# Turning the last row block of the MLP's input by transposing DMAs, in two halves of its columns

## The chip, the core and the metric

The kernel runs on one core of a Trainium2 chip. The metric is the time of one execution on the device in microseconds (us); shorter is better. An engine does its instructions in a fixed order, which is set when the kernel is built. TensorE (PE in the profile) multiplies, with its weight loads shown apart as PEld; VectorE is DVE, ScalarE is ACT, GpSimd is POOL, and SyncE (SP) issues most of the DMAs. "SPq" and "POOLq" mark the issuing side of a DMA.

## The reference

One layer of an encoder on 512 tokens of 1024 channels in float32: two attention branches, a gated merge, an output projection and a layer norm, then a gated MLP with a causal convolution of width 3. The change lies at the border between the first norm and the MLP:

```python
x = layer_norm(DEEPNORM_ALPHA * x + merged @ w_out[layer], ln1_g[layer], ln1_b[layer])
u, g = jnp.split(x @ w_ffn_in[layer], 2, axis=-1)
h = jax.nn.gelu(causal_dwconv(u, conv_w[layer], conv_b[layer])) * g
x = layer_norm(DEEPNORM_ALPHA * x + h @ w_ffn_out[layer], ln2_g[layer], ln2_b[layer])
```

## The kernel before

**Split products.** Every float32 matrix that is multiplied is held as a high part rounded to TensorE's fast float32 form (names ending in `h` or `hi`) and a low part, the rest (`l`, `lo`). A product is three matmuls: high by high, high by low, low by high. The high part is a ScalarE copy, the low part a VectorE subtraction.

**The border.** The output projection `out_proj` (lines 862 to 872) and the norm `first_norm` (lines 874 to 884) go over four row blocks of 128 tokens, j = 0 to 3, with tokens on the partitions. The MLP wants channels on the partitions: `x1h` and `x1l` hold the turned input, 8 chunks of 128 channels by 512 tokens. So each block has to be transposed.

Blocks 0 to 2 are turned by DMAs. A transposing DMA here takes 2-byte elements, so `send` (lines 903 to 910) copies the upper and the lower 16 bits of each number apart into `own` (two ScalarE copies of 128 x 1024) and SyncE issues one transposing DMA for each into `got`. `join` (lines 912 to 919) puts the halves of the numbers together in `back` (two ScalarE copies), and splits it into `x1h` (ScalarE) and `x1l` (VectorE). Block j is joined while the next block is projected.

Block 3 has no next block. `turn(3)` (lines 886 to 896) transposes it by eight TensorE matmuls against the identity (line 892) into two PSUM tiles `xt_ps`, and `x1h` and `x1l` are split straight from there.

**The MLP.** Its input weights come in 44 pieces of 128 output channels: u0, g0, u1, g1, ... (`f` counts them, u and g of one `f` belong together). A piece is 8 chunks x 3 matmuls = 24 matmuls of 512 tokens (`ffn_in`, lines 936 to 942). A piece's weights are loaded by SyncE into one of three raw tiles, and split into one of three pairs `whi`, `wlo` by ScalarE (line 104) and VectorE (line 113); a pair comes free when the piece has been multiplied. `activate(f)` evacuates u (ScalarE), convolves it (VectorE, lines 985 to 987), applies the GELU (ScalarE) and multiplies by g (VectorE). After every second `f` `first_products` begins the second matrix product, in accumulators P, Q and R, with weight pieces dx and dy that VectorE first adds and subtracts (lines 963 to 966).

Since block 3 comes last, the MLP starts on tokens 0 to 255 (`t_lo`), which need blocks 0 and 1 only: u0 whole, then six chunks of g0, then the transposes of block 3, two chunks of g0, and then u0 and g0 on tokens 256 to 511 (`t_hi`). u1 and all later pieces take 512 tokens at once. A program that simulates the times orders the instructions of each engine within the dependencies; `issue_after` ties one instruction behind another.

After the norm of block 3 has read its scale and offset, GpSimd loads those of the second norm into the same two tiles (`ln2` and `ln3`, line 828, 512 KB each).

Of the kernel before, what the change touches and what calls it, by code (L numbers as in the profile page):

```python
# [48 lines left out]
def r32(ap):  # L49
    return ap.bitcast(F32)  # L50
# [77 lines left out]
def tile_block(ctx: ExitStack, tc: tile.TileContext, xT, xN, w_qi, w_ki, w_t, w_v, w_br, w_o, w_fi, w_fo,  # L128
               bg, cw, rel, onehot, lnp, out):
    nc = tc.nc  # L130

    def close(p):
        p.__exit__(None, None, None)
# [69 lines left out]
    st = Stream(tc, rawp, ring, order, 3, 3, place, POOL_LO, DMA_LO)  # L203
# [4 lines left out]
    ps = pb("idle_ps")  # L208
# [4 lines left out]
    ident = cst.tile([128, 128], F32, name="ident")  # L213
# [86 lines left out]
    for k in range(KC):  # L300
# [9 lines left out]
        for n in range(4):  # L310
            c = slice(n * 128, n * 128 + 128)
# [360 lines left out]
    for a, b in ((0, 512), (512, NREL)):  # L672
        ps = pa("line_ps")
# [136 lines left out]
    for p in range(4):  # L810
        wh_wl = st.get(f"ba{p}")
        for n in (2 * p, 2 * p + 1):
            if n not in early and n not in gps:
                gps[n] = whole(proj_t(f"ga{n}"))
            ps = pb("ba_ps")
            wh, wl = wh_wl
            for k in range(4):
                c = slice((n % 2) * 512 + k * 128, (n % 2) * 512 + k * 128 + 128)
# [21 lines left out]
    def norm_apply(dst, r, mv, rstd, g, b, c):  # L840
        nc.vector.scalar_tensor_tensor(dst[:, c], r[:, c], mv[:, 0:1], g[:, c], op0=ALU.subtract, op1=ALU.mult)
        return nc.vector.scalar_tensor_tensor(dst[:, c], dst[:, c], rstd, b[:, c], op0=ALU.mult, op1=ALU.add).ins


    g1, b1 = bcast(0, "lg"), bcast(1, "lb")
# [8 lines left out]
    x1 = [dp.tile([128, D], F32, tag="r", bufs=NB, name=f"r{j}") for j in range(NB)]  # L854
# [3 lines left out]
    x1h = qp.tile([128, KC, S], F32R, name="x1h")  # L858
    x1l = qp.tile([128, KC, S], F32R, name="x1l")
# [14 lines left out]
    def first_norm(j, pss):  # L874
        r = x1[j]
        parts = padded(dp, [128, 2, 6], tag="parts", bufs=2, name="parts")
        for nh in range(2):
            c = slice(nh * 512, nh * 512 + 512)
            nc.vector.scalar_tensor_tensor(r[:, c], r[:, c], ALPHA, pss[nh], op0=ALU.mult, op1=ALU.add)
            nc.vector.bn_stats(parts[:, nh], r[:, c])  # L880
        mv, rstd = norm_stats(r, parts)
        for nh in range(2):
            last = norm_apply(r, r, mv, rstd, g1, b1, slice(nh * 512, nh * 512 + 512))
        return last

    def turn(j):
        t0 = slice(j * 128, j * 128 + 128)
        for nh in range(2):
            ps = pb("xt_ps")
            for k in range(4):  # L890
                kk = nh * 4 + k
                turned_last = nc.tensor.transpose(ps[:, k * 128:k * 128 + 128], x1[j][:, kk * 128:kk * 128 + 128], ident)
            src = ps.rearrange("p (k t) -> p k t", k=4)
            nc.scalar.activation(x1h[:, nh * 4:nh * 4 + 4, t0], src, AF.Copy)
            nc.vector.tensor_sub(x1l[:, nh * 4:nh * 4 + 4, t0], src, r32(x1h[:, nh * 4:nh * 4 + 4, t0]))
        return turned_last.ins

    tpc, tp = open_pool("tp", reuse_waits="tile")

    def halves_of(t):  # L900
        return t.bitcast(U16).rearrange("p (c two) -> p two c", two=2)

    def send(j):
        own = tp.tile([128, 2, D], U16, tag="own", bufs=1, name=f"own{j}")
        got = tp.tile([128, 2, KC, 128], U16, tag="got", bufs=1, name=f"got{j}")
        src = halves_of(x1[j])
        for a in (1, 0):
            nc.scalar.activation(own[:, a], src[:, a], AF.Copy)
            nc.sync.dma_start_transpose(got[:, a], own[:, a])
        return got  # L910

    def join(j, got):
# [17 lines left out]
    ec, ep = open_pool("ep", reuse_waits="tile")  # L930
# [5 lines left out]
    def ffn_in(w, ps, c, chunks=range(KC), lows_last=0):  # L936
        wh, wl = w
        terms = [(k, a, b) for k in chunks for a, b in ((wh, x1h), (wh, x1l), (wl, x1h))]
        terms.sort(key=lambda t: (t[0] >= lows_last, t[2] is x1l and t[0] < lows_last))
        for n, (k, a, b) in enumerate(terms):  # L940
            nc.tensor.matmul(ps[:, c], a[:, k * 128:k * 128 + 128], b[:, k, c], start=(k == 0 and a is wh and b is x1h),  # L941
                             stop=(n == len(terms) - 1 and k == KC - 1))
# [37 lines left out]
    def activate(f, ups, gps_):  # L980
        u = padded(fp, [128, S + 2], tag="u", bufs=2, name="u")
        nc.gpsimd.memset(u[:, 0:2], 0.0)  # L982
        nc.scalar.activation(u[:, 2:S + 2], ups, AF.Copy)
        c = fp.tile([128, S], F32, tag="c", bufs=2, name="c")
        nc.vector.tensor_scalar(c, u[:, 0:S], cwt[:, f, 0:1], None, op0=ALU.mult)
        nc.vector.scalar_tensor_tensor(c, u[:, 1:S + 1], cwt[:, f, 1:2], c, op0=ALU.mult, op1=ALU.add)
        nc.vector.scalar_tensor_tensor(c, u[:, 2:S + 2], cwt[:, f, 2:3], c, op0=ALU.mult, op1=ALU.add)  # L987
        nc.scalar.activation(c, c, AF.Gelu_apprx_tanh, bias=cwt[:, f, 3:4])  # L988

        if f % 2 == 0:  # L990
            hidden["F"] = hp.tile([128, 7, 256], F32, tag="F", bufs=1, name="hF")
            hidden["a"] = (hp.tile([128, 3, 256], F32R, tag="ah", bufs=1, name="ah"),
                           hp.tile([128, 3, 256], F32R, tag="al", bufs=1, name="al"))
        F = hidden["F"]
        o = 2 + 2 * (f % 2)
        nc.vector.tensor_mul(F[:, o:o + 2].rearrange("p a b -> p (a b)"), gps_, c)  # L996
        ah, al = hidden["a"]
        if f % 2 == 0:
            nc.scalar.activation(ah[:, 2], F[:, 2], AF.Copy)
            nc.vector.tensor_sub(al[:, 2], F[:, 2], r32(ah[:, 2]))  # L1000
            return
        nc.vector.tensor_add(F[:, 0], F[:, 3], F[:, 5])
        nc.vector.tensor_sub(F[:, 1], F[:, 0], F[:, 2])
        nc.scalar.activation(ah[:, 0:2], F[:, 0:2], AF.Copy)
        nc.vector.tensor_sub(al[:, 0:2], F[:, 0:2], r32(ah[:, 0:2]))
        nc.vector.tensor_sub(F[:, 3], F[:, 2], F[:, 3])
        nc.vector.tensor_sub(F[:, 6], F[:, 4], F[:, 1])
        bh = ep.tile([128, 4, 256], F32R, tag="bh", bufs=NP, name=f"bh{f//2}")
        bl = ep.tile([128, 4, 256], F32R, tag="bl", bufs=NP, name=f"bl{f//2}")
        nc.scalar.activation(bh, F[:, 3:7], AF.Copy)  # L1010
        nc.vector.tensor_sub(bl, F[:, 3:7], r32(bh))
        if f < FC - 1:
            first_ops.append((ah, al))
        rest_ops.append((bh, bl))
# [19 lines left out]
    early_w = {}  # L1034

    full, t_lo, t_hi = slice(0, S), slice(0, 256), slice(256, 512)
    w0 = [st.get("u0"), st.get("g0")]
    ps0 = [pa("u_ps"), pa("g_ps")]
    ffn_in(w0[0], ps0[0], t_lo)
    ffn_in(w0[1], ps0[1], t_lo, range(6))  # L1040
    with tc.issue_after(turn(NB - 1)):
        ffn_in(w0[1], ps0[1], t_lo, range(6, KC))
    ffn_in(w0[0], ps0[0], t_hi, lows_last=4)
    ffn_in(w0[1], ps0[1], t_hi)
    u1_ps = pa("u_ps")
    ffn_in(st.get("u1"), u1_ps, full)
    activate(0, *ps0)
    g1_ps = pa("g_ps")
    ffn_in(st.get("g1"), g1_ps, full)
    activate(1, u1_ps, g1_ps)  # L1050
    close(ac)
    psc, psC = open_pool("psC", space=PSUM, reuse_waits="tile")
    psd, psD = open_pool("psD", space=PSUM, reuse_waits="tile")
# [8 lines left out]
    for f in range(2, FC):  # L1062
        ups = bank_c("u_ps")
        ffn_in(st.get(f"u{f}"), ups, full)
        if f % 2 == 0:
            i = f // 2 - 1
            early_w[i] = st.get(f"dx{i}"), st.get(f"dy{i}")
            if i == 0:
                Q += [pb(f"Q{a}") for a in range(2)]
                R += [pb(f"R{a}") for a in range(2)]  # L1070
            first_products(i, (P, Q, R))
            if i < NB:
                nc.scalar.activation(x1[i], x1[i], AF.Copy, scale=ALPHA)
# [81 lines left out]
    i = NP - 1  # L1155
# [148 lines left out]
```

## Time and profile before

| | |
|---|---|
| median of three runs | 744.62 us (744.21 to 745.03) |
| profiled execution | 744.63 us |
| its span, first to last instruction | 742.8 us |
| mean granted TensorE clock | 0.998 |
| TensorE busy | 734.1 us, 99% of the span |
| VectorE, ScalarE, GpSimd busy | 570.8, 407.4, 150.2 us |
| DMA traffic | 117.03 MB |

The rows of a timeline give start and duration of an instruction in us, the engine, the line of the kernel, the operation, what it writes and from what, the shape, and in brackets the idle time of its engine before it and what ended it. Matmuls overlap: the time that one costs is the distance from its start to the next one's. The rows by tile give least, median and greatest duration in ns. A row of windows gives for a stretch the busy time of each engine, the granted clock, the mean busy share of the 16 DMA engines and GB/s.

### The profile page before, as it was taken

The page shows a single profiled execution, that of the slowest core. Times are in us where ns is not written, and L with a number is a line of the kernel's source. Part 1 is how long each engine was busy: PE and PEld are TensorE (multiplying, and loading weights), DVE is VectorE, ACT ScalarE, POOL GpSimd, SP SyncE. Part 2 cuts the span into 40 slices and gives each one's busy share as a digit, 9 for nine tenths or more (in the row PEclk, how much of TensorE's full clock was granted, in tenths as well). Part 3 has the DMA queues.
Part 4 walks back from the last instruction along what each step waited for, and adds up shares of the span by engine and source line. Part 5 has one row for each costly group of instructions (what it writes and reads, how often), then busy time and mean ns, then how long its engine had stood idle before and what let it go on. Part 6 is the DMA issues. An engine that isn't in the chain of part 4 may idle for free.

```text
span 742.8 us, 9709 instructions
## 1 busy us (share of the span) xinstructions
PE 734.1 (99%) x3453; PEld 615.3 (83%) x3453; DVE 570.8 (77%) x907; ACT 407.4 (55%) x572; POOL 150.2 (20%) x161
## 2 busy tenths in 40 slices
PE   9999999999999999999999999999999999999995
PEld 7888888888888888888889888888888888888885
DVE  5569888999679898668856776686767677668985
ACT  6466867797685688755384443443344344345430
POOL 0001224365753341000101111011101101110011
PEclk9999999999999999999999999999999999999999
DMA  8445887797476454438633535344443444448532
GB/s 266 158 123 183 200 191 167 153 214 171 120 184 163 135 138 124 121 114 268 236 62 116 168 114 169 120 143 147 159 141 114 158 141 154 140 145 285 193 117 86
DMA packets 73631, 117.03 MB, mean 158 GB/s; under 512 B 42536, under 2 KB 42792, under 8 KB 73584
## 3 DMA queue, kind: packets, MB, share of 16 engines
q1 hardware_dynamic: 66304, 93.98, 42.0%
q0 software_dynamic: 5744, 18.38, 9.9%
q10 hardware_dynamic: 1536, 4.06, 2.1%
q8 instruction: 27, 0.44, 0.2%
q14 instruction: 20, 0.16, 0.1%
HBM read 95.93 MB, written 9.98 MB: 143 GB/s over the span
## 4 chain that ended last, share of the span: by engine, by line
PE 98%; DVE 1%; issue 0%; DVEq 0%
PE u_ps L941 16%; PE g_ps L941 16%; PE av_ps L512 3%; PE m L1021 2%; PE m L1022 2%; PE m L1020 2%; PE ga_ps L234 2%; PE ga_ps L235 2%; PE ga_ps L233 2%; PE gb_ps L235 2%; PE gb_ps L233 2%; PE gb_ps L234 2%; PE o_ps L870 2%; PE o_ps L869 2%; PE o_ps L868 2%; PE z_ps L540 1%
## 5 line engine op out<-in xcount | busy, mean ns | idle before, releaser
L104 ACT ACTIVATE whi<-raw 128x1024 fp32r<-128x1024 f32 (+1 forms) x124 | 123.6, 1000 | 141.5 <-PE g_ps L941 45.0
L113 DVE TENSOR_TENSOR wlo<-raw,whi 128x1024 fp32r<-128x1024 f32 (+1 forms) x105 | 123.3, 1177 | 39.2 <-ACT whi L104 38.5
L941 PE MATMUL g_ps<-x1h,whi 128*128 128x512 f32 (+1 forms) x184 | 70.0, 380 | 0.0
L941 PE MATMUL g_ps<-x1l,whi 128*128 128x512 f32 (+1 forms) x184 | 69.9, 380 | 0.0
L941 PE MATMUL g_ps<-x1h,wlo 128*128 128x512 f32 (+1 forms) x184 | 69.9, 380 | 0.0
L941 PE MATMUL u_ps<-x1h,wlo 128*128 128x512 f32 (+1 forms) x184 | 69.8, 380 | 0.0
L941 PE MATMUL u_ps<-x1h,whi 128*128 128x512 f32 (+1 forms) x184 | 69.7, 380 | 0.0
L941 PE MATMUL u_ps<-x1l,whi 128*128 128x512 f32 (+1 forms) x184 | 69.3, 380 | 0.0
L941 PEld LDWEIGHTS u_ps<-x1h,wlo 128*128 128x128 f32 x184 | 34.6, 188 | 6.6
L941 PEld LDWEIGHTS g_ps<-x1l,whi 128*128 128x128 f32 x184 | 34.6, 188 | 6.6
L941 PEld LDWEIGHTS g_ps<-x1h,wlo 128*128 128x128 f32 x184 | 34.6, 188 | 6.6
L941 PEld LDWEIGHTS g_ps<-x1h,whi 128*128 128x128 f32 x184 | 34.6, 188 | 6.5
L941 PEld LDWEIGHTS u_ps<-x1h,whi 128*128 128x128 f32 x184 | 34.6, 188 | 6.4
L941 PEld LDWEIGHTS u_ps<-x1l,whi 128*128 128x128 f32 x184 | 34.4, 188 | 6.7
L963 DVE TENSOR_TENSOR t<-raw 128x512 f32<-128x512 f32 x11 | 7.6, 692 | 37.0 <-DMA raw<-in_w_fo_dram 37.0
L569 POOL TENSOR_TENSOR bm<-win,score 128x256 f32<-128x256 f32 (+2 forms) x24 | 28.9, 1229 | 31.9 <-DMA pl<-bm 21.8
L996 DVE TENSOR_TENSOR hF<-g_ps,c 128x512 f32<-128x512 f32 x22 | 15.1, 688 | 21.9 <-PE g_ps L941 21.1
L988 ACT ACTIVATE c<-c,cwt 128x512 f32<-128x512 f32 x22 | 15.9, 724 | 29.0 <-DVE c L987 28.8
L982 POOL MEMSET u<- 128x2 f32 x22 | 2.1, 98 | 147.3 <-ACT whi L104 111.1
L837 POOL TENSOR_TENSOR rstd<-rstd,mhalf 128x1 f32<-128x1 f32 x8 | 7.7, 958 | 104.5 <-DVE rstd L836 104.5
L424 DVE MAX8 m<-score 128x8 f32<-128x256 f32 (+2 forms) x48 | 26.6, 556 | 1.0
L557 POOL TENSOR_TENSOR beta<-beta,keep 128x1280 f32<-128x1280 f32 x8 | 21.0, 2626 | 26.9 <-DVE keep L554 26.9
(576 smaller groups left out, 2086.6 us busy)
## 6 DMA issues: line engine op xcount, KB each, us to landing
raw<-in_w_fi_dram SPq DMA_DIRECT2D x44, 512.0 KB, 3.3
raw<-in_w_t_dram SPq DMA_DIRECT2D x32, 512.0 KB, 3.8
raw<-in_w_fo_dram SPq DMA_DIRECT2D x26, 512.0 KB, 3.8
wlo<-in_w_t_dram POOLq DMA_DIRECT2D x14, 512.0 KB, 5.9
raw<-in_w_br_dram SPq DMA_DIRECT2D x8, 512.0 KB, 3.7
raw<-in_w_o_dram SPq DMA_DIRECT2D x8, 512.0 KB, 3.6
raw<-in_w_v_dram SPq DMA_DIRECT2D x7, 512.0 KB, 4.4
raw_b<-in_w_fo_dram SPq DMA_DIRECT2D x6, 512.0 KB, 4.2
```

The source lines that it names most:

```text
L104: self.high = nc.scalar.activation(hi[:, :w], t[:, :w], AF.Copy).ins
L113: self.done[key] = eng.tensor_sub(lo[:, :w], t[:, :w], r32(hi[:, :w])).ins
L233: nc.tensor.matmul(ps[:M], wh[:, c], xh[k], start=(k == 0), stop=False)
L234: nc.tensor.matmul(ps[:M], wh[:, c], xl[k], start=False, stop=False)
L235: ups["proj"] = nc.tensor.matmul(ps[:M], wl[:, c], xh[k], start=False, stop=(k == KC - 1)).ins
L424: nc.vector.max(m8, sc)
L512: nc.tensor.matmul(dst, vt[i][:, h].rearrange("p a d -> p (a d)"), t, start=(n == 0), stop=(n == len(seq) - 1))
L557: nc.gpsimd.tensor_mul(beta, beta, keep[:, 1:ATT + 1])
L569: nc.gpsimd.tensor_add(bm[:, OFF[j]:OFF[j] + N], win[:, 512 - N:512], score[j])
L941: nc.tensor.matmul(ps[:, c], a[:, k * 128:k * 128 + 128], b[:, k, c], start=(k == 0 and a is wh and b is x1h), stop=(n == len(terms) - 1 a ...
L988: nc.scalar.activation(c, c, AF.Gelu_apprx_tanh, bias=cwt[:, f, 3:4])
L996: nc.vector.tensor_mul(F[:, o:o + 2].rearrange("p a b -> p (a b)"), gps_, c)
```

## The change

Block 3 is now turned by transposing DMAs as well, in two halves of 512 columns. `first_norm` finishes the first half of the columns and hands it to `send_half`, then the second. `send_half` copies the upper 16 bits by ScalarE and the lower ones by VectorE and issues two transposing DMAs of 128 x 512. `join_half` puts a half together (the upper bits by ScalarE, the lower by VectorE) and splits it into four chunks of `x1h` and `x1l`.

u0, g0 and u1 now all take tokens 0 to 255 first, and then tokens 256 to 511, chunks 0 to 3 of all three before chunks 4 to 7. So u1 is 48 matmuls of 256 tokens in place of 24 of 512.

```diff
         mv, rstd = norm_stats(r, parts)
-        for nh in range(2):
-            last = norm_apply(r, r, mv, rstd, g1, b1, slice(nh * 512, nh * 512 + 512))
+        cols = [slice(nh * 512, nh * 512 + 512) for nh in range(2)]
+        if j < NB - 1:
+            for c in cols:
+                last = norm_apply(r, r, mv, rstd, g1, b1, c)
+            return last
+        for c in cols:
+            nc.vector.scalar_tensor_tensor(r[:, c], r[:, c], mv[:, 0:1], g1[:, c], op0=ALU.subtract, op1=ALU.mult)
+        last = None
+        for nh, c in enumerate(cols):
+            with tc.issue_after(last) if last is not None else nullcontext():
+                nc.vector.scalar_tensor_tensor(r[:, c], r[:, c], rstd, b1[:, c], op0=ALU.mult, op1=ALU.add)
+            last = send_half(j, nh)
         return last
...
+    def send_half(j, nh):
...
+        nc.scalar.activation(own[:, 1, c], src[:, 1, c], AF.Copy)
+        low = nc.vector.tensor_copy(own[:, 0, c], src[:, 0, c]).ins
+        for a in (1, 0):
+            nc.sync.dma_start_transpose(got[:, a, 4 * nh:4 * nh + 4], own[:, a, c])
+        return low
+
+    def join_half(j, nh, got, back, after):
...
+            nc.scalar.activation(halves_of(raw)[:, 1], got[:, 1, k].rearrange("p b c -> p (b c)"), AF.Copy)
+            nc.vector.tensor_copy(halves_of(raw)[:, 0], got[:, 0, k].rearrange("p b c -> p (b c)"))
+        src = raw.rearrange("p (k t) -> p k t", k=4)
+        high = nc.scalar.activation(x1h[:, k, t0], src, AF.Copy).ins
+        low = nc.vector.tensor_sub(x1l[:, k, t0], src, r32(x1h[:, k, t0])).ins
+        return high, low
...
-    w0 = [st.get("u0"), st.get("g0")]
-    ps0 = [pa("u_ps"), pa("g_ps")]
-    ffn_in(w0[0], ps0[0], t_lo)
-    ffn_in(w0[1], ps0[1], t_lo, range(6))
-    with tc.issue_after(turn(NB - 1)):
-        ffn_in(w0[1], ps0[1], t_lo, range(6, KC))
-    ffn_in(w0[0], ps0[0], t_hi, lows_last=4)
-    ffn_in(w0[1], ps0[1], t_hi)
-    u1_ps = pa("u_ps")
-    ffn_in(st.get("u1"), u1_ps, full)
-    activate(0, *ps0)
+    w0 = [st.get(t) for t in ("u0", "g0", "u1")]
+    ps0 = [pa(f"{t}_ps") for t in ("u", "g", "u")]
+    for w, ps in zip(w0, ps0):
+        ffn_in(w, ps, t_lo)
+    for chunks in (range(4), range(4, KC)):
+        for n, (w, ps) in enumerate(zip(w0, ps0)):
+            ffn_in(w, ps, t_hi, chunks, lows_last=4 if n == 0 else 0)
+    activate(0, *ps0[:2])
```

**The order on TensorE, where the tokens 256 to 511 begin.** Before; whi_3460 and wlo_3461 are u0's weights, whi_3466 g0's, whi_3472 and wlo_3473 u1's:

```order
L941 MATMUL g_ps<-x1h,wlo_3467 128x256
L892 MATMUL xt_ps<-ident,r_3479 128x128 x8
L941 MATMUL g_ps<-x1h,whi_3466 128x256
L941 MATMUL g_ps<-x1l,whi_3466 128x256
L941 MATMUL g_ps<-x1h,wlo_3467 128x256
```

In the changed kernel, at the first matmul that reads block 3 (the second row) and a little behind it:

```order
L972 MATMUL u_ps<-x1h,wlo_3473 128x256
L972 MATMUL u_ps<-x1h,whi_3460 128x256
L972 MATMUL u_ps<-x1h,wlo_3461 128x256
L972 MATMUL u_ps<-x1h,whi_3460 128x256
L972 MATMUL u_ps<-x1h,wlo_3461 128x256
L972 MATMUL u_ps<-x1h,whi_3460 128x256
L972 MATMUL u_ps<-x1h,wlo_3461 128x256
L972 MATMUL u_ps<-x1h,whi_3460 128x256
L972 MATMUL u_ps<-x1h,wlo_3461 128x256
L972 MATMUL g_ps<-x1h,whi_3466 128x256
L972 MATMUL u_ps<-x1h,whi_3472 128x256
L972 MATMUL u_ps<-x1l,whi_3460 128x256 x4
```

Before, the transposes stood inside g0's work on tokens 0 to 255. Now none are left, u1's work on these tokens stands ahead, and the first ten matmuls on tokens 256 to 511 read `x1h` only.

**The order on SyncE**, with the semaphores that each issue waits for (own_3707... are block 2's, own_3775 block 3's):

```order
L907 DMA_TRANSPOSE got_3707<-own_3706 128x8x128 [waits DMAHW2_49,Activation_49]
L931 DMA_TRANSPOSE got_3776<-own_3775 128x4x128 [waits DMAHW2_49,DMAHW1_49,DMAHW3_49,DVE_49,Activation_49]
L931 DMA_TRANSPOSE got_3776<-own_3775 128x4x128 [waits DMAHW4_49,Activation_49]
L931 DMA_TRANSPOSE got_3776<-own_3775 128x4x128 [waits Activation_49]
L931 DMA_TRANSPOSE got_3776<-own_3775 128x4x128 [waits DVE_49]
L73 DMA raw_3995<-in_w_fo_dram 128x1024 [waits DVE_49]
```

Four issues stand between block 2's and the load of dy0. The first one waits for VectorE's copy, the second and third for ScalarE's, the fourth for VectorE's again.

**The order on VectorE behind the border.** Before, from u0's convolution (`c<-u`) to g1's product; raw_3966 is dy0:

```order
L985 TENSOR_SCALAR c<-u,cwt 128x512
L113 TENSOR_TENSOR wlo_3805<-raw_3802,whi_3804 128x1024
L986 SCALAR_TENSOR_TENSOR c<-u,cwt,c 128x512
L987 SCALAR_TENSOR_TENSOR c<-u,cwt,c 128x512
L963 TENSOR_TENSOR t_3970<-raw_3966 128x512
L965 TENSOR_TENSOR raw_3966<-raw_3966,raw_3921 128x512
L966 TENSOR_TENSOR raw_3966<-t_3970,raw_3921 128x512
L996 TENSOR_TENSOR hF<-g_ps,c 128x512
L113 TENSOR_TENSOR wlo_3924<-raw_3921,whi_3923 128x512
L985 TENSOR_SCALAR c<-u,cwt 128x512
L1000 TENSOR_TENSOR al<-hF,ah 128x256
```

In the changed kernel; raw_3995 is dy0:

```order
L113 TENSOR_TENSOR wlo_3830<-raw_3827,whi_3829 128x512
L1016 TENSOR_SCALAR c<-u,cwt 128x512
L1018 SCALAR_TENSOR_TENSOR c<-u,cwt,c 128x512
L994 TENSOR_TENSOR t_3999<-raw_3995 128x512
L1017 SCALAR_TENSOR_TENSOR c<-u,cwt,c 128x512
L996 TENSOR_TENSOR raw_3995<-raw_3995,raw_3827 128x512
L997 TENSOR_TENSOR raw_3995<-t_3999,raw_3827 128x512
L1027 TENSOR_TENSOR hF<-g_ps,c 128x512
L1018 SCALAR_TENSOR_TENSOR c<-u,cwt,c 128x512
L113 TENSOR_TENSOR wlo_3998<-raw_3995,whi_3997 128x1024
L1031 TENSOR_TENSOR al<-hF,ah 128x256
L1027 TENSOR_TENSOR hF<-g_ps,c 128x512
```

The steps on dy0 and u0's product `hF` now stand between the steps of u1's convolution, and dy0's low part ahead of `al`.

More of the change, by code (lines that the diff above doesn't have):

```diff
@@ L881, in first_norm @@
         mv, rstd = norm_stats(r, parts)
-        for nh in range(2):
-            last = norm_apply(r, r, mv, rstd, g1, b1, slice(nh * 512, nh * 512 + 512))
-        return last
[L886 to L896, printed above, removed]
+        cols = [slice(nh * 512, nh * 512 + 512) for nh in range(2)]
[10 more added lines that the diff above has]
+            last = send_half(j, nh)
+        return last
     tpc, tp = open_pool("tp", reuse_waits="tile")
@@ L919, in join @@
         nc.vector.tensor_sub(x1l[:, :, t0], src, r32(x1h[:, :, t0]))
+    sending = {}
+    def send_half(j, nh):
+        if not nh:
+            sending[j] = (tp.tile([128, 2, D], U16, tag="own", bufs=1, name=f"own{j}"),
+                          tp.tile([128, 2, KC, 128], U16, tag="got", bufs=1, name=f"got{j}"))
+        own, got = sending[j]
+        src = halves_of(x1[j])
+        c = slice(nh * 512, nh * 512 + 512)
+        nc.scalar.activation(own[:, 1, c], src[:, 1, c], AF.Copy)
[4 more added lines that the diff above has]
+    def join_half(j, nh, got, back, after):
+        t0 = slice(j * 128, j * 128 + 128)
+        k = slice(4 * nh, 4 * nh + 4)
+        raw = back[:, 512 * nh:512 * nh + 512]
+        with ExitStack() as ties:
+            for ins in after:
+                ties.enter_context(tc.issue_after(ins))
+            nc.scalar.activation(halves_of(raw)[:, 1], got[:, 1, k].rearrange("p b c -> p (b c)"), AF.Copy)
[4 more added lines that the diff above has]
+        return high, low
     for j in range(NB):
@@ L927, in tile_block @@
             got = send(j)
+    back = tp.tile([128, D], F32, tag="back", bufs=1, name=f"back{NB - 1}")
+    joined_last = ()
+    for nh in range(2):
+        joined_last = join_half(NB - 1, nh, sending[NB - 1][1], back, joined_last)
     close(tpc)
@@ L1036, in tile_block @@
     full, t_lo, t_hi = slice(0, S), slice(0, 256), slice(256, 512)
-    w0 = [st.get("u0"), st.get("g0")]
-    ps0 = [pa("u_ps"), pa("g_ps")]
-    ffn_in(w0[0], ps0[0], t_lo)
-    ffn_in(w0[1], ps0[1], t_lo, range(6))
-    with tc.issue_after(turn(NB - 1)):
-        ffn_in(w0[1], ps0[1], t_lo, range(6, KC))
-    ffn_in(w0[0], ps0[0], t_hi, lows_last=4)
-    ffn_in(w0[1], ps0[1], t_hi)
-    u1_ps = pa("u_ps")
-    ffn_in(st.get("u1"), u1_ps, full)
-    activate(0, *ps0)
+    w0 = [st.get(t) for t in ("u0", "g0", "u1")]
[6 more added lines that the diff above has]
+    activate(0, *ps0[:2])
     g1_ps = pa("g_ps")
     ffn_in(st.get("g1"), g1_ps, full)
-    activate(1, u1_ps, g1_ps)
+    activate(1, ps0[2], g1_ps)
     close(ac)
@@ L1072, in tile_block @@
             if i < NB:
-                nc.scalar.activation(x1[i], x1[i], AF.Copy, scale=ALPHA)
+                with tc.issue_after(joined_last[0]) if i == NB - 1 else nullcontext():
+                    nc.scalar.activation(x1[i], x1[i], AF.Copy, scale=ALPHA)
         if f == FC - 1:
```

## The prediction

> **What bounds the kernel now.** I read the page first, then TensorE's waits, then the timeline of the change's place, 388 to 422 us.
>
> ```profile
> span 742.8 us, 9709 instructions
> PE 734.1 (99%) x3453; PEld 615.3 (83%) x3453; DVE 570.8 (77%) x907; ACT 407.4 (55%) x572; POOL 150.2 (20%) x161
> PE idle_ps L210 <- DVE idle L207: 1.2, 1, 1.2
> ```
>
> The third line is the whole list of TensorE's waits: once, 1.2 us, at the start. After that TensorE is issuing all the time, so the time is the sum of its steps, and any gap that the change opens is paid in full. The steps are read from start to start:
>
> ```profile
> 388.96 0.28 PE L941 MATMUL u_ps<-x1h,whi 128*128 128x256 f32 x1
> ...
> 391.83 0.28 PE L941 MATMUL g_ps<-x1h,whi 128*128 128x256 f32 x1
> ...
> 393.99 1.04 PE L892 MATMUL xt_ps<-ident,r 128*128 128x128 f32 x8
> 394.78 0.36 PE L941 MATMUL g_ps<-x1h,whi 128*128 128x256 f32 x1
> 394.98 0.29 PE L941 MATMUL g_ps<-x1l,whi 128*128 128x256 f32 x1
> 395.11 0.28 PE L941 MATMUL g_ps<-x1h,wlo 128*128 128x256 f32 x1
> ...
> 404.12 0.39 PE L941 MATMUL u_ps<-x1h,whi 128*128 128x512 f32 x1
> ...
> 406.84 0.39 PE L941 MATMUL g_ps<-x1h,whi 128*128 128x512 f32 x1
> ```
>
> The 24 matmuls of u0 on tokens 0 to 255 take 391.83 - 388.96 = 2.87 us: 0.1197 us for a 256-wide one. Between 404.12 and 406.84 lie twelve 512-wide ones: 0.2267 us each. The row at 406.84 is the first matmul of g1; from there on the changed kernel issues nearly the same matmuls, so I carry the change to that row.
>
> **The change part by part.** *Removed:* the eight TensorE transposes. 393.99 to 394.78 is 0.79 us, and the two matmuls behind start 0.20 and 0.13 us apart where 0.12 is normal: 0.88 us gone. *Split:* u1's 24 matmuls of 512 become 48 of 256: 24 x (2 x 0.1197 - 0.2267) = +0.31 us. TensorE's own steps thus fall by 0.57 us; nothing else shortens the path.
>
> *Moved:* before, block 3 needed the transposes, and the rest of g0's low-token work and the x1h split were fitted around them with no wait. Now TensorE does u0, g0 and u1 on tokens 0 to 255, 72 x 0.1197 = 8.62 us from 388.96, and at 397.58 needs x1h of block 3, columns 0 to 511. When is it there?
>
> ```profile
> 390.92 1.40 DVE L841 SCALAR_TENSOR_TENSOR r<-r,mv,ln 128x512 f32<-128x512 f32 x2
> 392.24 1.41 DVE L842 SCALAR_TENSOR_TENSOR r<-r,rstd,ln 128x512 f32<-128x512 f32 x2
> L842 DVE SCALAR_TENSOR_TENSOR r<-r,rstd,ln x14: 743/748/752, 365.5 to 734.3; 128x512 f32<-128x512 f32 x14
> L477 DVE COPY bm<-lg x8: 806/818/844, 202.4 to 296.9; 128x1280 uint16<-128x1280 uint16 x8
> L908 ACT ACTIVATE own<-r x6: 1040/1048/1061, 366.9 to 383.8; 128x1024 uint16<-128x1024 uint16 x6
> L909 SPq DMA_TRANSPOSE got<-own x6: 1232/1260/1293, 368.0 to 385.2; - x6
> L479 SPq DMA_TRANSPOSE pl<-bm x16: 1259/1346/1608, 203.1 to 299.3; - x16
> ```
>
> The first half of the normalised block ends at 392.24 + 0.75 = 392.99. The low halves are copied by VectorE: the nearest row is 0.82 us for 1280 columns, so about 0.36 us for 512, done at 393.40 with a hop. ScalarE copies the high halves beside it: 1.05 us for 1024, about 0.6 for 512, done at 393.6. SyncE issues four transposing DMAs one after the other, and by the waits in the new order the low one of the first half goes first: 393.45. What one issue holds SyncE is the first unknown. The rows have 1.26 us for 1024 columns and 1.35 (least 1.26) for 1280: hardly anything for 25% more columns. I take 1.2 us for 512; its bounds are 0.63 (all of it goes with the width) and 1.26 (none). So the second issue starts at 394.65; the copies of the other half are ready by then.
>
> ```profile
> DMA to landing us min/median/max: 3.1/3.2/3.3
> 369.00:372.00 3.00, 3.00 (x15) 2.48 (x14) 2.86 (x6) 1.74 (x2) 0.99 (x1) 1.00 0.93 175
> 394.00:399.00 5.00, 5.00 (x44) 4.96 (x43) 2.07 (x3) 2.03 (x3) 0.62 (x3) 1.00 0.67 205
> 392.62 0.58 POOL L828 DMA_DIRECT2D ln<-in_lnp_dram  x1 [0.55 <-DVE r L841]
> 393.95 0.53 POOL L828 DMA_DIRECT2D ln<-in_lnp_dram  x1 [0.74 <-DVE r L842]
> pl<-bm SPq DMA_TRANSPOSE x16, 3.5
> pl<-keep SPq DMA_TRANSPOSE x8, 4.5
> DMA to landing us min/median/max: 3.4/3.6/6.8
> ```
>
> The landing is the second unknown. The first line is that of the six transposes of blocks 0 to 2, 3.2 us. The next shows their work on the DMA engines (last but one number, the share of 16 engines): 0.93 of 3 us for two of them, 1.4 us each. Half the data is 0.7 us less, so 2.5 us on idle engines. But these engines aren't idle here: GpSimd issues the two 512 KB loads of ln2 and ln3 (the two L828 rows), and with them alone the engines are busy 0.67 of 394 to 399 us, where blocks 0 to 2 had nothing beside them. The 1280-wide transposes land in 3.5 us at the median in one stage and in 4.5 in a busier one, at most 6.8 (the last line is theirs). I take 3.2 us: half the data won, about as much lost to the loads. Bounds 1.9 (issue and data halved) and 6.8. The fixed part doesn't shrink with the half, and four issues stand where two would do.
>
> The Trainium skill (DMA: Bandwidth & Descriptors, Anatomy of one DMA — SWDGE (gpsimd) path) prices a DMA at about 2.0 us fixed plus its bytes at 436 GB/s, which speaks against halves too. By that, an estimate, a half of 128 KB lands in 2.3 us and a whole transpose in 2.6, where the row has 3.2 for the whole; with 2.3 in place of 3.2 the sum below would be +0.2 us.
>
> ```profile
> L916 ACT ACTIVATE back<-got x6: 1338/1359/1379, 371.3 to 388.4; 128x1024 uint16<-128x1024 uint16 x6
> L894 ACT ACTIVATE x1h<-xt_ps x2: 593/595/597, 394.6 to 395.1; 128x512 fp32r<-128x512 f32 x2
> ```
>
> The second DMA (high halves) lands at 394.65 + 3.2 = 397.85. Behind it stand ScalarE's copy into `back`, half of 1.36 us, and the x1h split, 0.6 us, with three hops of 0.05: x1h is there at 399.30. VectorE's low copy waits for the first DMA, a step earlier, and is covered. **TensorE stands 399.30 - 397.58 = 1.72 us.** Block 2's x1l comes later than now but before that. The second half comes two issues later, 2.4 us; from 399.30 TensorE has 36 matmuls, 4.3 us, so it is covered.
>
> *Sum:* -0.88 + 0.31 + 1.72 = +1.15 us. The same by the row of g1: 399.30 + 72 x 0.1197 = 407.92 against 406.84, +1.08. I take +1.1 us: the profiled execution, 744.63 us around a span of 742.8, becomes 745.7. The median of the three runs is 744.62, the same for this purpose. With the bounds: landing 2.5 gives +0.4, everything halved no wait and -0.6, landing 4.5 +2.4, 6.8 +4.7.
>
> *Behind it.* u0, g0 and u1 now end within 2.6 us of each other, just ahead of g1; before, u0 ended 6 us ahead of it. What hangs on their ends comes later against TensorE:
>
> ```profile
> 400.56 1.06 ACT L104 ACTIVATE whi<-raw 128x1024 fp32r<-128x1024 f32 x1 [3.90 <-PE u_ps L941]
> 402.90 0.34 SPq L73 DMA_DIRECT2D raw<-in_w_fo_dram  x1
> 408.94 1.40 DVE L113 TENSOR_TENSOR wlo<-raw,whi 128x512 fp32r<-128x512 f32 x1
> 416.63 0.69 DVE L1005 TENSOR_TENSOR al<-hF,ah 128x512 fp32r<-128x512 f32 x1
> 418.88 1.22 DVE L113 TENSOR_TENSOR wlo<-raw,whi 128x1024 fp32r<-128x1024 f32 x1
> 419.99 0.62 PE L1022 MATMUL Q<-whi,al 128*128 128x512 f32 x2
> 422.26 0.39 PE L941 MATMUL g_ps<-x1h,wlo 128*128 128x512 f32 x1
> ```
>
> The first row is g1's weight split, which waits for u0's ring slot; g1 followed 6.3 us after it began. Now u0's last matmul is about 22 matmuls, 2.6 us, ahead of g1. The split's two steps (1.06 and 1.22 us) still fit, by 0.5 us as g1's third matmul is the first that needs the low part. The load of dy0 (402.90) waits for that split, so it is issued near 407.7, and VectorE's three steps on dy0 fall between the convolutions of u0 and u1. Before, `al` was done 2.7 us ahead of the Q matmul that reads it (417.32 against 419.99) and g2's low weights 2.2 us ahead of theirs (420.10 against 422.26). Laid out in the new order of VectorE with the same durations, I get 0.9 and 0.8 us of margin left, and 0.1 to 0.2 if one step runs beside a GpSimd step as the 1.40 us row does (0.7 us more than its size gives). I cost it at nothing; without that cover it is 0.3 to 1 us. Later, u3 and dx1 have over 2 us to spare.
>
> **The rivals.** Within 0.2%, 1.49 us, a measurement of this kernel can't tell a change from none.
>
> *A, the forecast:* a gap of 1 to 2 us in front of the high tokens, more than the 0.57 us won: 745.7, from 745.0 to 746.1. For it: the transposes' chain is a sum of measured rows. Against it: two of its rows are for other widths.
>
> *B, the DMA engines decide:* the halves share them with ln2 and ln3, whose issue hardly moves (the first waits for the L841 rows). A landing of 4.5 us, the `pl<-keep` row, gives 399.30 + 1.3 = 400.6 and +2.4 us: 747.1, slower; at 6.8 us it is 749.3. It decides from a landing of 3.6 us on, where the gap passes 2.1 us. For it: the share of 0.67, and 4.5 against 3.5 us for the same transfer in two stages. Against it: half the data, and the engines are not full.
>
> *C, no gap:* the issue goes with the width (0.63 us) and the landing is 1.9 us; x1h is there at 394.08 + 1.9 + 1.45 = 397.43, before TensorE asks. Then the time is 744.63 - 0.6 = 744.0, the side of a gain, though too small to be told. Against it: the issue row at 1280 columns, whose least value is that at 1024.
>
> *D, the thin margins behind break:* A's gap and 0.3 to 1 us more at Q or g2: 746.0 to 746.7, on either side of the bound.
>
> **How the numbers follow.** A 0.50, B 0.27, C 0.11, D 0.12. A and C and a third of D lie within 0.2% with a few of A's runs above it: 0.60 same, 0.38 slower. A gain of more than 1.49 us has no source here, since TensorE's own steps fall by 0.57 us only: 0.02. The predicted time is A's, 745.7. The range takes in C almost whole and B up to a landing of about 5.3 us (+3.2 us): 744.2 to 747.9.
>
> **What would show it.** In the profile of the changed kernel: no transposing matmul; TensorE's list of waits gains one row, u_ps waiting for ScalarE's x1h, near 397.6 us and of 1 to 2 us (right), none (C), or over 2.1 us (B, with got's landings above 3.6 us); SyncE's four issues near 1.2 us each; g1's first matmul near 407.9 in place of 406.84, and the rest of the program shifted by the same amount. A second wait at Q or at g2's low weights is D. The forecast is wrong if TensorE's busy steps outside the gap move by more than 0.3 us from -0.57, or if the end shifts by something else than g1's start.

## The result: 1.0% slower

The changed kernel takes 751.68 us at the median of five runs (750.91 to 753.37), the kernel before beside it 744.62 us (744.08 to 745.03): a ratio of 1.0101, interval 1.0084 to 1.0118. The forecast was 745.7 us with a range of 744.2 to 747.9; the time lies above the range, on the side to which 0.38 was given.

The profiled execution took 753.31 us. From the page of the changed kernel, its first lines, and the whole list of TensorE's waits (total, times, longest, in us):

```profile
span 751.4 us, 9760 instructions
PE 737.2 (98%) x3469; PEld 619.0 (82%) x3469; DVE 572.3 (76%) x911; ACT 410.0 (55%) x576; POOL 149.1 (20%) x161
PE u_ps L972 <- ACT x1h L944: 5.5, 1, 5.5
PE idle_ps L210 <- DVE idle L207: 1.2, 1, 1.2
PE m L1051 <- DVE hF L1027: 0.2, 1, 0.2
```

The span is 8.6 us longer than before. The list gained the row that the forecast named, u_ps waiting for ScalarE's x1h, but at 5.5 us in place of 1 to 2. TensorE's busy time *rose* by 3.1 us, though its steps should have shrunk by 0.57: that is the second surprise. Both are seen in TensorE's timeline:

```profile
389.36 0.28 PE L972 MATMUL u_ps<-x1h,whi 128*128 128x256 f32 x1
...
397.87 0.28 PE L972 MATMUL u_ps<-x1h,wlo 128*128 128x256 f32 x1
403.70 0.58 PE L972 MATMUL u_ps<-x1h,whi 128*128 128x256 f32 x1 [5.55 <-ACT x1h L944]
404.07 0.41 PE L972 MATMUL u_ps<-x1h,wlo 128*128 128x256 f32 x1
404.29 0.41 PE L972 MATMUL u_ps<-x1h,whi 128*128 128x256 f32 x1
...
409.62 0.28 PE L972 MATMUL u_ps<-x1h,whi 128*128 128x256 f32 x1
...
415.02 0.40 PE L972 MATMUL g_ps<-x1h,whi 128*128 128x512 f32 x1
```

From the first matmul on tokens 0 to 255 (389.36) to the last (397.87) 71 steps take 8.51 us, 0.12 each as before. TensorE is ready again at 397.99 and goes on at 403.70: 5.71 us from step to step. Then the same 256-wide matmul costs 0.21 us, not 0.12, up to 409.62: 27 matmuls in 5.92 us where 27 x 0.1197 = 3.23 is normal, 2.69 us lost. From 409.62 the step is 0.12 again. The windows of this stretch say why (length, then busy us and instructions of TensorE, its weight loads, VectorE, ScalarE, GpSimd, then granted clock, DMA share, GB/s):

```profile
394.00:398.00 4.00, 4.00 (x35) 3.94 (x33) 2.13 (x3) 0.69 (x2) 0.67 (x3) 1.00 1.10 197
398.00:402.00 4.00, 0.15 (x2) 0.00 (x0) 0.21 (x1) 0.00 (x0) 0.00 (x0) 1.00 1.03 168
402.00:406.00 4.00, 2.30 (x11) 2.31 (x12) 1.82 (x4) 3.25 (x5) 0.00 (x0) 0.60 0.14 30
406.00:410.00 4.00, 4.00 (x22) 4.00 (x22) 0.19 (x1) 0.41 (x1) 0.00 (x0) 0.55 0.00 0
```

TensorE's mean granted clock is 0.60 and 0.55 of full speed in the two windows behind the gap; it comes back after 409.6. And from 394 to 402 us the DMA share is 1.10 and 1.03 (the row adds up the times of all packets, so it can pass 1). The chain to x1h, row by row (SyncE's four issues by tile, the second one alone, the landing of the four, ScalarE's two steps on the first half):

```profile
L931 SPq DMA_TRANSPOSE got<-own x4: 1190/1264/1347, 394.0 to 397.9; - x4
395.26 1.22 SPq L931 DMA_TRANSPOSE got<-own  x1
DMA to landing us min/median/max: 5.1/6.5/7.7
402.21 0.77 ACT L941 ACTIVATE back<-got 128x512 uint16<-128x512 uint16 x1 [6.98 <-DMA got<-own]
403.01 0.63 ACT L944 ACTIVATE x1h<-back 128x512 fp32r<-128x512 f32 x1
```

The second transpose is issued at 395.26, and ScalarE, idle for 6.98 us, can copy it at 402.21: 6.9 us from issue to landing. What stands ahead of it and behind it is as forecast to 0.2 us. What else the DMA engines did is in the page's queue rows, asked for single microseconds (packets, MB, share of 16 engines). q0 carries the two loads ln2 and ln3, which GpSimd issues at 393.02 and 394.87, q1 the transposes. The first pair of rows is the microsecond from 396 to 397, the second that from 401 to 402; the last row is the issue of ln3, with the time to its landing at the end:

```profile
q0 software_dynamic: 38, 0.12, 74.3%
q1 hardware_dynamic: 344, 0.09, 73.0%
...
q1 hardware_dynamic: 756, 0.18, 134.4%
q0 software_dynamic: 3, 0.00, 0.2%
...
ln<-in_lnp_dram POOLq DMA_DIRECT2D x1, 512.0 KB, 6.8
```

And the same for the four microseconds from 397 to 401 in one:

```profile
q0 software_dynamic: 132, 0.48, 67.9%
q1 hardware_dynamic: 582, 0.14, 35.7%
```

ln3 lands at 394.87 + 6.8 = 401.7. From 397 to 401 the transposes move 0.14 MB; as soon as ln3 is done, they move 0.18 MB in one microsecond. The four of them, 0.5 MB in all, were issued over 3.9 us and land within 1.4 us, from 401.7 (393.98 + 7.7) on, with the load or behind it.

**The account at g1's first matmul**, from u0's: 415.02 - 389.36 = 25.66 us, against 406.84 - 388.96 = 17.88 before: +7.78. The terms are -0.88 (transposes) + 0.31 (u1 in halves) + 5.71 (gap) + 2.69 (low clock) = +7.83. The rest of the 8.6 us: u0 began 0.40 later in this execution, and 0.4 us come behind g1, of which the wait at L1051, far behind, is 0.2. One execution is profiled, and the five range over 2.5 us; the profiled one is 1.6 us above the median, so the terms are those of a long run.

### The profile page after: what moved, and what is told of

It reads as the page before. It is cut to its first block, busy times and chain, and to the rows that moved or that the text cites. A ratio compares the mean times of both kernels' runs of the same rounds, so it can differ in the third digit from the quotient of the medians.

```text
span 751.4 us, 9760 instructions
## 1 busy us (share of the span) xinstructions
PE 737.2 (98%) x3469; PEld 619.0 (82%) x3469; DVE 572.3 (76%) x911; ACT 410.0 (55%) x576; POOL 149.1 (20%) x161
## 4 chain that ended last, share of the span: by engine, by line
PE 93%; DVE 3%; DMA 2%; ACT 1%; issue 0%; DVEq 0%; ACTq 0%
PE u_ps L972 15%; PE g_ps L972 14%; PE av_ps L512 3%; PE m L1051 2%; PE m L1052 2%; PE m L1053 2%; PE ga_ps L234 2%; PE ga_ps L235 2%; PE ga_ps L233 2%; PE gb_ps L235 2%; PE gb_ps L233 2%; PE gb_ps L234 2%; PE o_ps L870 2%; PE o_ps L869 2%; PE o_ps L868 2%; PE z_ps L540 1%
## 5 line engine op out<-in xcount | busy, mean ns | idle before, releaser
L972 PE MATMUL u_ps<-x1h,whi 128*128 128x512 f32 (+1 forms) x192 | 72.1, 376 | 5.5 <-ACT x1h L944 5.5
L972 PE MATMUL u_ps<-x1h,wlo 128*128 128x512 f32 (+1 forms) x192 | 71.9, 375 | 0.0
L972 PE MATMUL u_ps<-x1l,whi 128*128 128x512 f32 (+1 forms) x192 | 71.3, 375 | 0.0
L972 PEld LDWEIGHTS u_ps<-x1h,whi 128*128 128x128 f32 x192 | 36.9, 192 | 12.0 <-ACT x1h L944 5.8
L972 PEld LDWEIGHTS u_ps<-x1h,wlo 128*128 128x128 f32 x192 | 36.9, 192 | 6.2
L972 PEld LDWEIGHTS u_ps<-x1l,whi 128*128 128x128 f32 x192 | 36.5, 192 | 6.3
```

## Experiments

Two explanations of the late landing stood against each other. T1: the loads ln2 and ln3 hold the transposes up on the DMA engines that they share. T2: transposes of half the width, four issues in place of two, are slow by themselves. The low clock was taken to follow from the gap. Two sets of kernels were timed, each on one chip, with the kernel before beside them: 745.16 us (744.17 to 747.42) for the four that follow the change in the table, 744.86 us (744.09 to 745.42) for the last four. All edits are against the changed kernel. The gap and the landing are those of the one profiled execution. There were two executions of filler20, four of whole, filler and ln2_late, five of the change and ten or eleven of the others.

| kernel | median us | ratio to before | interval | gap, us | landing of the last transposes, min/median/max |
|---|---|---|---|---|---|
| the change | 751.68 | 1.0101 | 1.0084 to 1.0118 | 5.5 | 5.1/6.5/7.7 |
| ln_late | 746.00 | 1.002 | 1.0011 to 1.003 | 1.1 | 2.4/2.5/3.2 |
| ln3_late | 746.68 | 1.002 | 1.001 to 1.003 | 1.8 | 2.5/3.1/3.9 |
| whole | 752.37 | 1.0104 | 1.0089 to 1.0119 | 5.4 | 5.5/5.8/6.0 |
| filler | 749.64 | 1.0066 | 1.005 to 1.0083 | none | 4.0/5.5/6.0 |
| ln2_late | 749.85 | 1.0069 | 1.0055 to 1.0083 | 4.0 | 2.4/4.1/5.3 |
| filler20 | 750.25 | 1.0072 | 1.0053 to 1.009 | 2.4 | 4.5/5.7/6.8 |
| merged | 745.13 | 1.0006 | 0.9997 to 1.0016 | 0.8 | 3.2/3.2/3.3 |
| hybrid | 744.63 | 0.9996 | 0.9988 to 1.0005 | none | 2.4/2.4/2.4 |

### ln_late: both loads behind the transposes

```diff
-    g2, b2 = bcast(2, "lg"), bcast(3, "lb")
...
-                nc.gpsimd.tensor_sub(x[:, 512:1024], x[:, 512:1024], t[:, 512:1024])
+                hidden["sub"] = nc.gpsimd.tensor_sub(x[:, 512:1024], x[:, 512:1024], t[:, 512:1024]).ins
...
             if i == 0:
+                with tc.issue_after(hidden["sub"]):
+                    g2, b2 = bcast(2, "lg"), bcast(3, "lb")
```

> The changed kernel with the two loads of ln2 and ln3 issued about 25 us later on GpSimd, behind the first subtraction of dx0, when the transposes are long done. Theory 1 (the two loads hold the transposes up on the shared DMA engines): the halves land in 2.5 to 3.2 us, TensorE's gap falls from 5.5 us to 1.0 to 1.8 us, the granted clock stays at 1.00, and the time is 744.62 + 0.4 to 1.2 = 745.0 to 745.8 us. Theory 2 (four issues of half the width are slow by themselves): landings stay at 5 to 7 us, the gap at 5 us, the time at 751 to 752 us.

The profile of this kernel: the four issues with their landing, the windows of the gap and behind it, the first matmul on tokens 256 to 511 with its wait, and g1's first:

```profile
L931 SPq DMA_TRANSPOSE got<-own x4: 1190/1242/1314, 393.7 to 397.5; - x4
DMA to landing us min/median/max: 2.4/2.5/3.2
398.00:402.00 4.00, 3.03 (x25) 3.03 (x26) 1.82 (x3) 3.00 (x5) 0.00 (x0) 1.00 0.35 40
402.00:406.00 4.00, 4.00 (x35) 4.00 (x35) 0.03 (x1) 1.11 (x2) 0.00 (x0) 1.00 0.00 0
398.97 0.39 PE L971 MATMUL u_ps<-x1h,whi 128*128 128x256 f32 x1 [1.12 <-ACT x1h L944]
407.70 0.40 PE L971 MATMUL g_ps<-x1h,whi 128*128 128x512 f32 x1
```

With the loads away the same four half-width transposes land in 2.5 us, the gap is 1.1 us, the clock stays at 1.00, and g1 begins 407.70 - 389.05 = 18.65 us after u0 (17.88 before, so +0.77). The ratio falls from 1.0101 to 1.002. T1 stands and T2 falls, by this alone. It is also the kernel that the prediction described: a gap of 1 to 2 us and a loss of 0.2%, 0.84 us.

### ln3_late and ln2_late: which of the two loads

ln3_late moves only ln3 to the later place, ln2_late only ln2. What stays in front is, in ln3_late:

```diff
-    g2, b2 = bcast(2, "lg"), bcast(3, "lb")
+    g2 = bcast(2, "lg")
```

and in ln2_late:

```diff
-    g2, b2 = bcast(2, "lg"), bcast(3, "lb")
+    b2 = bcast(3, "lb")
```

> As ln_late, but ln2 is loaded where it was and only ln3 later, so that one of the two loads of 512 KB stands beside the transposes. Theory 1: a part of the wait is left, as the second transpose lands about 4.5 us after its issue (half of the way between 2.5 and 6.8), the gap is near 3 us and the clock may or may not drop: 746.5 to 749 us. Theory 2: as the changed kernel, 751 to 752 us.

> The changed kernel with only ln2 loaded late and ln3 where it was. With ln3 late alone the gap was 1.8 us, with both late 1.1, with neither 5.5. If the number of loads beside the transposes decides, this gives 1.8 us again and about 746.5 us. If it is the load that is issued in the middle of the transposes (ln3, 0.9 us behind the first one's issue), the gap is 3 us or more and the time 748 us or more.

In ln3_late the load that is left is issued 1.0 us ahead of the first transpose; in ln2_late, where it waits for the norm's last step L892, 0.9 us behind it. From the timelines of GpSimd, the tables by tile and the lists of DMA issues (the load with its landing), first of ln3_late:

```profile
392.49 0.58 POOL L828 DMA_DIRECT2D ln<-in_lnp_dram  x1 [0.55 <-DVE r L888]
L931 SPq DMA_TRANSPOSE got<-own x4: 1190/1256/1265, 393.4 to 397.3; - x4
ln<-in_lnp_dram POOLq DMA_DIRECT2D x1, 512.0 KB, 4.3
```

and of ln2_late:

```profile
396.00 0.58 POOL L828 DMA_DIRECT2D ln<-in_lnp_dram  x1 [2.39 <-DVE r L892]
L931 SPq DMA_TRANSPOSE got<-own x4: 1191/1251/1291, 395.1 to 399.0; - x4
ln<-in_lnp_dram POOLq DMA_DIRECT2D x1, 512.0 KB, 4.3
```

One load of the same size costs a gap of 1.8 us where it is ahead of the transposes (0.7 more than with no load) and 4.0 us where it comes in their midst. ln3_late's gap was expected too large, near 3 us; ln2_late's is the second case of its expectation. So it isn't the number of loads alone but the time of the load. It lands at 392.49 + 4.3 = 396.8 in ln3_late, a little before the second transpose would have landed by itself, and at 396.00 + 4.3 = 400.3 in ln2_late. There the first transpose, issued ahead of the load, lands in 2.4 us; the three behind it land later than 400.3, the first of them at 401.7.

ln3_late has a second thing to teach: its profiled execution kept the clock at 1.00, but three of its ten executions (747.13, 747.49 and 747.85 us) have a mean granted clock of 0.995, like all four of ln2_late, and the other seven (745.96 to 747.50 us) one of 0.997 or 0.998. That the clock fell in those three too, behind a gap of this size, is likely; no trace of them shows it.

ln2_late's profile has one more wait of 1.3 us, for a weight piece well ahead of the change, which belongs to no edit here.

### whole: two issues of the full width

```diff
-        for a in (1, 0):
-            nc.sync.dma_start_transpose(got[:, a, 4 * nh:4 * nh + 4], own[:, a, c])
+        if nh:
+            for a in (1, 0):
+                nc.sync.dma_start_transpose(got[:, a], own[:, a])
```

> The changed kernel with block 3 sent in two transposing DMAs of the whole width once both halves are copied, as blocks 0 to 2 are; the joins, the order of the matmuls and the loads of ln2 and ln3 stay. Theory 1 (the loads hold the transposes up): they land as late as now, 5 to 7 us after their issue, and the gap is 5 to 6.5 us: 751 to 753 us. Theory 2 (the halves are slow): they land in 3.2 to 3.6 us, x1h is there near 401.5 us, the gap is 3.5 to 4 us: 747.5 to 750 us.

Block 3 goes in two transposes of 1024 columns, with the loads where the change has them. 752.37 us, a gap of 5.4 us: the same as with halves, as T1 expected. The number and the width of the transposes don't decide, which rules T2 out a second time. The issue of ln3, the two transposes and ln3's landing:

```profile
395.01 0.53 POOL L828 DMA_DIRECT2D ln<-in_lnp_dram  x1 [1.26 <-DVE r L892]
L932 SPq DMA_TRANSPOSE got<-own x2: 1232/2348/3465, 395.2 to 396.6; - x2
ln<-in_lnp_dram POOLq DMA_DIRECT2D x1, 512.0 KB, 5.2
```

Here no load is issued between the transposes: both stand ahead of them, ln3 by 0.2 us. So a place in their midst isn't needed. ln3 lands at 395.01 + 5.2 = 400.2, and the transposes at 401.3 and 402.1. The traces of all six kernels with a load in front (the change, whole, filler, filler20, ln2_late, ln3_late) agree on one thing: every transpose of block 3 that was issued while such a load was on its way landed after that load, by 0.4 us or more.

### filler: no gap for TensorE

44 matmuls of 256 columns into an accumulator that nobody reads are put between tokens 0 to 255 and 256 to 511: work that is added, in the place of the gap.

```diff
+    spare = pb("spare_ps")
+    for _ in range(44):
+        with tc.issue_after(filled):
+            filled = nc.tensor.matmul(spare[:, t_lo], w0[0][0][:, 0:128], x1h[:, 0, t_lo], start=True, stop=True).ins
```

> The changed kernel with 44 extra matmuls of 256 columns into a PSUM tile that nobody reads, placed between the low and the high tokens, 44 x 0.12 = 5.3 us: TensorE works where it stood. The transposes are not touched. If the lowered clock after the gap (28 matmuls at 0.2135 us, +2.6 us) is a consequence of the idle time, the clock stays at 1.00 and the time falls from 751.7 to about 749.0 us. If the clock drops for another reason, the time stays at 751.7 us.

From its timeline and windows:

```profile
397.36 5.44 PE L1076 MATMUL spare_ps<-x1h,whi 128*128 128x256 f32 x44
402.64 0.28 PE L972 MATMUL u_ps<-x1h,whi 128*128 128x256 f32 x1
402.00:406.00 4.00, 4.00 (x36) 4.00 (x34) 1.76 (x3) 2.38 (x4) 0.00 (x0) 1.00 0.01 4
```

TensorE has no gap and the clock stays at 1.00; the time over the kernel before falls from 751.68 - 744.62 = 7.1 us to 749.64 - 745.16 = 4.5 us, although the transposes still land in up to 6.0 us. So the low clock is the consequence of TensorE standing still: the 2.7 us that it costs are a part of their own, and the 4.5 us that are left are the late landing.

### filler20: a shorter gap

The same with 20 matmuls that nobody reads.

```diff
-    for _ in range(44):
+    for _ in range(20):
```

> As filler, with 20 extra matmuls in place of 44: TensorE stands idle for 5.5 - 2.4 = 3.1 us (2.5 to 3.5 as the landing varies). If the clock drops only behind a longer idle time, it stays at 1.00 and the time is that of filler, 749 to 750 us; if every gap of 3 us drops it, the clock falls to 0.56 for about 6 us behind it and the time is 751 to 752 us.

The added matmuls, the first matmul behind them with its wait, and the next one:

```profile
397.84 2.56 PE L1076 MATMUL spare_ps<-x1h,whi 128*128 128x256 f32 x20
402.78 0.58 PE L972 MATMUL u_ps<-x1h,whi 128*128 128x256 f32 x1 [2.39 <-ACT x1h L944]
403.16 0.42 PE L972 MATMUL u_ps<-x1h,wlo 128*128 128x256 f32 x1
```

A gap of 3.1 us was meant; it came out at 2.4 us, and the clock fell all the same: 0.38 us from 402.78 to 403.16, and then steps of 0.21. The two executions of filler20 lie 2.9 us apart (748.82 and 751.68, the profiled one, which has another wait of 0.8 us at 439.61, far behind), so its time only says that it is slower than before.

### merged: both planes of a half in one transposing DMA

The loads are late as in ln_late, and `own` is laid out so that one DMA sends the high and the low halves of 512 columns:

```diff
-        for a in (1, 0):
-            nc.sync.dma_start_transpose(got[:, a, 4 * nh:4 * nh + 4], own[:, a, c])
+        nc.sync.dma_start_transpose(got[:, nh].rearrange("p a b c -> p (a b) c"), own[:, nh].rearrange("p a c -> p (a c)"))
```

> The changed kernel with the late loads, and with both 16-bit planes of a half in one transposing DMA of 128 x 1024 columns: two issues in place of four. If the serial issue of 1.2 us on SyncE sets the remaining gap of 1.1 us, one issue less stands ahead of the first half, while its landing grows from 2.5 to 3.2 us: the gap is 0.5 us, and the time 0.5 to 0.6 us below that of ln_late, that is 0.2 to 0.3 us above the kernel before. If the data or the receipt sets it, the gap stays at 1.1 us or grows.

Two issues, 1.23 and 1.29 us, each landing in 3.2 us; the gap is 0.8 us (expected 0.5) and g1 comes 18.32 us after u0, +0.44 against ln_late's +0.77. One issue less ahead of x1h saves 1.26 us, 0.7 of it go to the longer landing (3.2 against 2.5); of the 0.6 left, 0.3 arrived. The difference to before can't be told: 1.0006 (0.9997 to 1.0016).

### hybrid: half by TensorE, half by DMA

The loads are late; the first 512 columns are turned by four TensorE matmuls inside g0, the other half by two transposing DMAs; u1 takes 512 tokens again.

```diff
+    def turn_half(j):
...
+        for k in range(4):
+            last = nc.tensor.transpose(ps[:, k * 128:k * 128 + 128], x1[j][:, k * 128:k * 128 + 128], ident)
...
+    ffn_in(w0[0], ps0[0], t_lo)
+    ffn_in(w0[1], ps0[1], t_lo, range(5))
+    with tc.issue_after(turn_half(NB - 1)):
+        ffn_in(w0[1], ps0[1], t_lo, range(5, KC))
```

> With the loads of ln2 and ln3 late: the first half of block 3's columns is turned by four TensorE transposes, the second half by two transposing DMAs, and u1 is split by chunks (0 to 3, then 4 to 7) at 512 tokens in place of by tokens. Theory 1: four of eight transposes are saved (0.44 us), u1 costs no extra step, the second half's x1h is there near 400 us and is asked for near 400.8 us, so no gap: 0.4 us faster than the kernel before, 0.06%, which can't be told from no change. Theory 2 (DMA transposes of half the width are slow): a gap of 2 us or more, slower by 1.5 us or more.

No gap; g1 begins 406.09 - 388.65 = 17.44 us after u0, 0.44 less than before, which is half of the eight transposes: the TensorE side of the sum holds to the hundredth. In the time it doesn't show: 0.9996 (0.9988 to 1.0005). No version here is measurably faster than the kernel before; the most that this idea can win is the 0.57 to 0.88 us of TensorE's steps, below 0.2%.

## Why the prediction was wrong

**Right.** *Removed and split.* Change: -0.88 and +0.31 us close the account to 0.05 us, and hybrid has its half. *Issue.* 1.2 us was taken for 512 columns; it took 1.19 to 1.35. The second issue was forecast 394.65 - 388.96 = 5.69 us after u0, and came 5.90 after it. *From landing to TensorE* 1.45 us was forecast; from 402.16, a hop ahead of ScalarE's copy, to 403.70 it is 1.54. *The second half* is covered: its `x1h` never stops TensorE. *Behind it.* The low parts for Q and g2 stop nothing; the first of `al`'s last steps ends at 427.41, 0.3 us ahead of the matmul that reads it:

```profile
426.72 0.69 DVE L1036 TENSOR_TENSOR al<-hF,ah 128x512 fp32r<-128x512 f32 x1
427.74 0.39 PE L1053 MATMUL Q<-whi,al 128*128 128x512 f32 x1
```

So D did not happen, though the margin is thinner than the 0.9 us forecast. C, no gap at all, failed in both its terms: the issue does not go with the width, and the landing was 2.4 us at least, with the engines idle too, in place of 1.9.

**Wrong, first: the term "I take 3.2 us: half the data won, about as much lost to the loads".** The landing was 6.90 us, 3.70 more; with 0.21 of the issue and 0.09 behind it the gap becomes 1.72 + 4.00 = 5.72, which is the 5.71 measured. Rival B had the mechanism and, as its far end, even the size (6.8 us, +4.7 us). It got 0.27, "half the data, and the engines are not full". That was read from a mean share of 0.67 over five microseconds. The question to ask of the rows was *which load is on its way when a transpose is issued, and when it lands*: the prediction quotes ln3's issue at 393.95, ahead of its own second transpose at 394.65, and the list of DMA issues before has ln3's landing 5.2 us later, at 399.1. A second transpose that lands there or later means, with the 1.45 us behind it, a gap of some 3 us at the least. That it was 5.7 comes mostly from ln3 itself: issued 0.5 us later against u0 than before (it waits for the norm's last step, which now stands behind a copy, where B said "hardly moves"), it took 6.8 us to land in place of 5.2. By ln_late the estimate for idle engines, 2.5 us, was exact; with the loads in front the landing lay at the upper bound, 6.8, and not at the middle.

**Wrong, second: a term that no case had.** The forecast and all rivals let TensorE go on at full speed behind the gap. Behind a long gap it does not: +2.69 us. B's far end of 749.3 us with this added is 752.0; the measured median is 751.68 and the profiled execution 753.31. The forecast's own condition for being wrong, TensorE's steps outside the gap moving by more than 0.3 us from -0.57, was met by this.

With only the first error the change would have been 744.63 - 0.57 + 5.71 = 749.8 us, the neighbourhood of filler's 749.64; with neither, ln_late's 746.0, inside the range.

**Open.** Why ln3 holds the transposes back, rather than sharing the engines by halves, is not shown: the queue rows tell that it does (0.14 MB in 4 us), not which part of the engines decides so. That a transpose lands behind the load that was issued ahead of it is an order seen in these six traces, not a mechanism; no run moved a load in small steps. Nor is it shown why the first transpose, issued 0.9 us ahead of ln3, waits for it too in the change (7.7 us) and in filler20 (6.8), and not in filler (4.0).

## What to carry to other kernels

Before a transfer is put on the path that sets the end, list the loads that are on their way when it is issued or are issued before it lands, look up when they land, and let it land behind them in the sum; a stage without such company does not give its landing. A mean DMA share below 1 does not say that a small transfer passes. And a gap of some 2 us or more on an otherwise gapless TensorE is to be priced with what follows it: here 5.7 us of waiting cost 8.4.

## What the hardware showed that was not expected

**The clock falls and rises in steps of 3.41 us.** In windows of 0.2 us the granted clock is either 1.00 or 0.50, and the two slices with a value between give its edges. The change: the fall, the rise, and the next fall, at the end of the program:

```profile
402.60:402.80 0.20, 0.00 (x0) 0.00 (x0) 0.00 (x0) 0.20 (x1) 0.00 (x0) 0.97 0.00 0
402.80:403.00 0.20, 0.00 (x0) 0.00 (x0) 0.00 (x0) 0.18 (x1) 0.00 (x0) 0.50 0.14 41
...
409.60:409.80 0.20, 0.20 (x4) 0.20 (x3) 0.00 (x0) 0.00 (x0) 0.00 (x0) 0.96 0.00 0
...
747.40:747.60 0.20, 0.00 (x0) 0.00 (x0) 0.20 (x2) 0.00 (x0) 0.00 (x0) 0.83 0.00 0
```

then ln2_late:

```profile
404.00:404.20 0.20, 0.20 (x3) 0.20 (x3) 0.20 (x1) 0.00 (x0) 0.00 (x0) 0.88 0.00 0
407.40:407.60 0.20, 0.20 (x3) 0.20 (x2) 0.00 (x0) 0.00 (x0) 0.00 (x0) 0.59 0.00 0
```

and filler20:

```profile
402.20:402.40 0.20, 0.00 (x0) 0.00 (x0) 0.00 (x0) 0.20 (x1) 0.00 (x0) 0.69 0.00 0
405.60:405.80 0.20, 0.20 (x3) 0.20 (x3) 0.00 (x0) 0.00 (x0) 0.00 (x0) 0.78 0.00 0
```

A mean of 0.97 over 0.2 us is a fall 0.01 us before its end, and so on: low from 402.79 to 409.62 in the change, 6.83 us; from 404.15 to 407.56 in ln2_late, 3.41 us; from 402.28 to 405.69 in filler20, 3.41 us. whole has 6.83 us again. And from the rise at 409.62 to the fall at 747.53 the change has 337.92 us, 99 times 3.413; in filler20, from 405.69 to 747.02, it is 341.33, 100 times. So the decision is taken once in 3.41 us, on a beat of its own: in ln2_late TensorE had been back at work for 0.9 us, at full speed, when the clock fell. In the change the fall came inside the gap and TensorE's return at 403.70 was too late for that beat, so it paid two. The price of a gap thus depends on where the beat lies, and the three executions of ln3_late with the lower mean clock fit that. From 1.8 us (no fall in ln3_late's profile) and 2.4 us (a fall in filler20) no threshold can be read, since the beat lay differently in each.

The Trainium skill (TensorE: Matmul & The Clock Gate, Part 1: The HAM clock gate) states this clock: half speed after an idle window of about 3.4 us, a window that runs freely. The length, the two levels and the free beat agree with the rows. That the window has to be idle does not: in filler20 TensorE worked until 400.39, about 1.5 of the 3.41 us that ended with the fall at 402.28.

**A transposing DMA's landing** of 2.5 us for 512 columns, and 3.2 us for 1024, on otherwise idle engines became 5.1 to 7.7 us in the change, with two 512 KB loads issued ahead of the second one. With one load, up to 5.3 us in ln2_late, where it is issued behind the first; 0.6 us more at the median (3.1) in ln3_late, where it is issued 1.0 us ahead of the first and lands early.
